# A rotary embedding on one core: two loads in halves, and VectorE's code on a block boundary

## The chip, the core and the metric

The kernel runs on one of the eight cores of a Trainium2 chip. A core has five engines that run their own instruction streams beside each other: TensorE (PE, matrix products), VectorE (DVE), ScalarE (ACT), GpSimd (POOL) and SyncE (SP, which here only issues transfers). Data moves between the chip's main memory (HBM) and the core's working memory (SBUF, 128 partitions) through 16 DMA engines that all queues share. The metric is the time of one execution on the device, in microseconds (us).

## What is computed

Each vector of 64 numbers is split into two halves, and the halves are rotated by a table of cosines and sines that depends on the position in the sequence:

```python
x: (8, 2048, 8, 64) float32;  cos, sin: (2048, 32) float32
x1, x2 = x[..., :32], x[..., 32:]
out1 = x1 * cos - x2 * sin
out2 = x1 * sin + x2 * cos
out = concatenate([out1, out2], axis=-1)
```

Input and output are 33.55 MB each, and each number is used once.

## The kernel before

The eight batches are numbered b0 to b7. One batch is a tile `xt` of 128 partitions with 8,192 numbers (32 KB) each: partition q holds 16 consecutive positions (`ROW`). A `UNIT` is a quarter of that, 2,048 numbers or 8 KB. Five such tiles exist (`NBUF`), the result is written over the input, and the tile is stored from there.

**Loads** are issued by SP (line 67, function `load`). Batch 0 comes in three transfers of 8, 8 and 16 KB per partition, the others in one of 32 KB. Lines 77 and 78 issue the loads of b0 to b4 at the start. The load of batch b+5 is issued after batch b has been worked on (line 195), into the tile that batch b used, and so waits until batch b's store has landed. A transfer is cut into rows, one for each partition, and each of the 16 DMA engines has 8 of them.

**Stores** (line 74, function `store`) are issued by ScalarE, for b7 by SP. Batch 0 is stored in three transfers of 4, 12 and 16 KB per partition, b7 in three of 16, 8 and 8 KB, the others in one of 32 KB (function `shares`).

**Work** is done in pieces of 8 KB per partition (two of 4 KB at either end, function `pieces`). `rotate` has three kinds of piece. Kind A, the usual one: GpSimd multiplies the swapped halves by the sines (line 124, two instructions), VectorE multiplies by the cosines (line 131) and adds both (line 138). Kind B, one piece in b2, b4 and b5: the addition is done by TensorE with an identity matrix (lines 145 and 146), and ScalarE copies the result back (line 147). Kind C, one piece in b1 and b3: VectorE also does the multiplication by the sines (line 150), without GpSimd. A piece waits for the transfer that holds it, so with a batch loaded in one transfer the first piece waits for all of it.

**Order.** `keep` holds each engine's instructions in the order of the program. The framework puts the semaphores: transfers take turns on eight of them, and a transfer that reuses one waits until the one before it on that semaphore has landed.

**Code alignment.** Lines 80 and 81 pad the instruction streams of VectorE and GpSimd ahead of their first own instruction, so that it stands at slot 120 of a block of 128 instruction slots:

```python
for eng in (nc.vector, nc.gpsimd):
    keep(eng.addr_align(128, offset=120))
```

Of the kernel before, what the change touches and what calls it, by code (L numbers as in the profile page):

```python
# [10 lines left out]
def kernel(  # L11
# [7 lines left out]
    nc = tc.nc  # L19
    keep = tc.keep_in_program_order  # L20
# [8 lines left out]
    ROW = R * HD  # L29
    UNIT = 4 * HD  # L30
# [27 lines left out]
    def spans(sizes):  # L58
        lo = 0
        for n in sizes:  # L60
            yield lo, n
            lo += n

    def load(b):
        xt = xpool.tile([P, ROW], f32, tag="xt", name=f"xt{b}")
        for lo, n in spans([UNIT, UNIT, 2 * UNIT] if b == 0 else [ROW]):
            keep(nc.sync.dma_start(out=xt[:, lo : lo + n], in_=xv[b, :, lo : lo + n]))  # L67
            if b == 0 and lo == 0:
                keep(nc.sync.dma_start(out=cos_sb, in_=cos_src))
        xts[b] = xt  # L70
# [6 lines left out]
    for b in range(NBUF):  # L77
        load(b)

    for eng in (nc.vector, nc.gpsimd):  # L80
        keep(eng.addr_align(128, offset=120))
    keep(nc.gpsimd.memset(eye, 0.0))  # L82
    nc.gpsimd.affine_select(
        out=eye,
# [101 lines left out]
    for b in range(B):  # L186
        done = 0
        outs = list(spans(shares(b)))
        for lo, n in spans(pieces(b)):
            rotate(b, lo, n)  # L190
            done = lo + n
            while outs and sum(outs[0]) <= done:
                store(b, *outs.pop(0))
        if b + NBUF <= last:
            load(b + NBUF)
# [30 lines left out]
```

## Time and profile before

| | |
|---|---|
| time, median of 3 runs | 163.67 us (163.3 to 163.88) |
| the profiled execution | 163.52 us, span 161.7 us |
| busy, share of the span | VectorE 87%, GpSimd 86%, TensorE 31%, ScalarE 8% |
| moved by the DMA engines | 67.65 MB, 418 GB/s over the span |
| load of a whole batch, issue to landing | 39.3 us (median of 7) |
| store of a whole batch, issue to landing | 29.2 us (median of 6) |
| VectorE: multiplication by cosines (line 131), addition (line 138) | 2167 and 2145 ns mean |
| GpSimd: one multiplication by sines (line 124) | about 2200 ns mean |

The span reaches from the first to the last instruction of the program on the core; the execution's time has 1.8 us around it. The profile is of one execution, so its parts add up to its own 163.52 us, not to the median. "q1" and "q10" are DMA queues, "q14" is the queue over which the engines' instructions are fetched. In the busy tenths a digit is the busy share of one of 40 equal slices of the span, 9 for 90% or more. A line of the waits reads: engine and line, what it waited for, microseconds in total, number of times, the longest. A line of the timeline or of the chain reads: start in us, duration in us, engine and line; a "q" behind an engine's name is its instruction that issues a transfer.

### The profile page before, as it was taken

To read this page: it belongs to the slowest core of one execution; us is meant where nothing else is said; L and a number is where in the kernel's file an instruction comes from. 1 tells how busy PE (TensorE), PEld (TensorE's weight loads), DVE (VectorE), ACT (ScalarE), POOL (GpSimd) and SP (SyncE) were. 2 spreads that over 40 slices of the span, in tenths; PEclk is the share of its full clock that TensorE was granted. 3 is DMA by queue.
4 is the path that set the end of the run, shared out by engine and by line. 5 is a ranking of instruction groups with operands and counts; after the bars stand their busy time and mean duration, and the time that the engine had idled before them with its cause. 6 is when DMAs were issued, how large, how long until landed. Compare 5 with 4: busy or idle time off the path is not lost.

```text
span 161.7 us, 565 instructions
## 1 busy us (share of the span) xinstructions
PE 50.1 (31%) x80; PEld 18.7 (12%) x80; DVE 140.1 (87%) x66; ACT 12.8 (8%) x14; POOL 138.9 (86%) x70
## 2 busy tenths in 40 slices
PE   0000000597309760978049724973000000000000
PEld 0000000142004220322023302320000000000000
DVE  0397999999999999999999999599989998999910
ACT  3300000002200220021100220022000000000000
POOL 1499996999999999995999979997999979999400
PEclk9999999999975998579956995599655555555555
DMA  5999999999999999999999999999999999999894
GB/s 181 421 434 450 411 429 425 414 417 483 393 405 454 450 446 397 454 446 397 454 446 397 446 454 397 446 454 397 454 446 397 446 454 397 454 454 421 385 422 207
DMA packets 3458, 67.65 MB, mean 418 GB/s; under 512 B 384, under 2 KB 384, under 8 KB 768
## 3 DMA queue, kind: packets, MB, share of 16 engines
q1 hardware_dynamic: 2016, 38.01, 55.4%
q10 hardware_dynamic: 1440, 29.62, 42.7%
q14 instruction: 2, 0.02, 0.0%
HBM read 34.08 MB, written 33.55 MB: 418 GB/s over the span
## 4 chain that ended last, share of the span: by engine, by line
DMA 47%; DVE 37%; POOL 9%; issue 2%; DVEq 0%; SPq 0%; POOLq 0%; ACTq 0%
DMA xt<-in_x_dram 24%; DMA out_dram<-xt 19%; DVE t L131 18%; DVE xt L138 17%; POOL t L124 9%; DMA sin_sb<-in_sin_dram 3%; DVE t L150 1%; DVEq L138 0%; SPq L67 0%; POOLq L124 0%; ACTq L74 0%
## 5 line engine op out<-in xcount | busy, mean ns | idle before, releaser
L124 POOL TENSOR_TENSOR t<-xt,sin_sb 128x1024 f32<-128x1024 f32 (+1 forms) x32 | 70.5, 2202 | 9.7 <-DMA xt<-in_x_dram 6.6
L131 DVE TENSOR_TENSOR t<-xt,cos_ps 128x2048 f32<-128x2048 f32 (+1 forms) x34 | 73.4, 2167 | 0.8
L124 POOL TENSOR_TENSOR t<-xt,nsin 128x1024 f32<-128x1024 f32 (+1 forms) x32 | 70.4, 2201 | 0.0
L138 DVE TENSOR_TENSOR xt<-t,t 128x2048 f32<-128x2048 f32 (+1 forms) x29 | 62.2, 2145 | 6.5 <-POOL t L124 4.0
L145 PE MATMUL o<-t,eye 128*128 128x512 f32 x24 | 17.5, 818 | 22.6 <-DVE t L131 19.2
L162 PE MATMUL o<-t,eye 128*128 128x512 f32 x16 | 12.2, 853 | 37.5 <-DVE t L131 35.3
L146 PE MATMUL o<-t,eye 128*128 128x512 f32 x24 | 14.9, 709 | 0.0
L147 ACT COPY xt<-o 128x1024 f32<-128x1024 f32 x6 | 6.1, 1012 | 45.7 <-PE o L146 45.7
L145 PEld LDWEIGHTS o<-t,eye 128*128 128x128 f32 x24 | 5.6, 256 | 32.0 <-issue 26.1
L162 PEld LDWEIGHTS o<-t,eye 128*128 128x128 f32 x16 | 3.7, 256 | 43.1 <-issue 39.1
L167 ACT COPY xt<-o 128x1024 f32<-128x1024 f32 x4 | 4.0, 1012 | 47.9 <-PE o L163 47.9
L146 PEld LDWEIGHTS o<-t,eye 128*128 128x128 f32 x24 | 5.7, 239 | 8.5 <-issue 8.0
L95 DVE COPY cos_ps<-cos_sb 128x512 f32<-128x512 f32 x1 | 0.7, 694 | 6.8 <-DMA cos_sb<-in_cos_dram 6.8
L163 PE MATMUL o<-t,neye 128*128 128x512 f32 x8 | 6.4, 894 | 0.2 <-DVE t L150 0.2
L150 DVE TENSOR_TENSOR t<-xt,sin_ps 128x2048 f32<-128x2048 f32 x2 | 4.6, 2282 | 0.0
L163 PE MATMUL o<-t,eye 128*128 128x512 f32 x8 | 4.1, 592 | 0.0
L163 PEld LDWEIGHTS o<-t,neye 128*128 128x128 f32 x8 | 2.2, 305 | 5.4 <-issue 3.8
L82 POOL MEMSET eye<- 128x128 f32 x1 | 0.2, 204 | 2.4 <-issue 2.4
L163 PEld LDWEIGHTS o<-t,eye 128*128 128x128 f32 x8 | 1.5, 190 | 1.9 <-issue 1.9
L92 ACT ACT_TABLE_LOAD x1 | 1.3, 1283 | 1.2 <-PEq L210 1.2
L92 ACT ACTIVATE nsin<-sin_sb 128x512 f32<-128x512 f32 x1 | 0.6, 630 | 3.9 <-DMA sin_sb<-in_sin_dram 3.9
L93 ACT COPY sin_ps<-sin_sb 128x512 f32<-128x512 f32 x1 | 0.6, 578 | 0.0
(6 smaller groups left out, 1.0 us busy)
## 6 DMA issues: line engine op xcount, KB each, us to landing
xt<-in_x_dram SPq DMA_DIRECT2D x7, 4096.0 KB, 39.3
out_dram<-xt ACTq DMA_DIRECT2D x6, 4096.0 KB, 29.2
xt<-in_x_dram SPq DMA_DIRECT2D x2, 1024.0 KB, 6.5
xt<-in_x_dram SPq DMA_DIRECT2D x1, 2048.0 KB, 12.7
out_dram<-xt ACTq DMA_DIRECT2D x1, 2048.0 KB, 26.6
out_dram<-xt SPq DMA_DIRECT2D x1, 2048.0 KB, 11.6
out_dram<-xt SPq DMA_DIRECT2D x2, 1024.0 KB, 8.0
out_dram<-xt ACTq DMA_DIRECT2D x1, 1536.0 KB, 21.5
```

The lines of the kernel that those rows point to most:

```text
L92: keep(nc.scalar.mul(nsin, sin_sb, -1.0))
L95: keep(nc.vector.tensor_copy(cos_ps, cos_sb))
L124: nc.gpsimd.tensor_mul(out=t2u[:, :, u, :].rearrange("p (r h) d -> p r h d", h=H), in0=xu[:, :, 1 - u, :].rearrange("p (r h) d -> p r h d" ...
L131: nc.vector.tensor_mul(out=t1.rearrange("p (r k d) -> p r k d", r=nr, d=Dh), in0=xk, in1=rep(cos_ps[:, r0 : r0 + nr, :], 2 * H),)
L138: keep(nc.vector.tensor_add(out=xt, in0=t1, in1=t2))
L145: nc.tensor.matmul(oc, eye, t1[:, cs], start=True, stop=False)
L146: nc.tensor.matmul(oc, eye, t2[:, cs], start=False, stop=True)
L147: keep(nc.scalar.copy(xt[:, 2 * j * C : 2 * (j + 1) * C], o))
L150: nc.vector.tensor_mul(out=t2.rearrange("p (r k d) -> p r k d", r=nr, d=Dh), in0=xk, in1=rep(sin_ps[:, r0 : r0 + nr, :], 2 * H),)
L162: nc.tensor.matmul(oc, eye, t1u[:, gs, u, :], start=True, stop=False)
L163: nc.tensor.matmul(oc, eye if u else neye, t2u[:, gs, 1 - u, :], start=False, stop=True)
L167: nc.scalar.copy(xu[:, :, u, :], o.rearrange("p (g d) -> p g d", d=Dh))
```

## The change

The loads of the second and third batch (b1 and b2) become two transfers each, one for the first and one for the second half of each partition's 32 KB, in this order on the same queue. The pieces of these batches are the same as before. VectorE's first own instruction is put at the start of a block of 128 slots instead of slot 120; GpSimd's stays at slot 120.

```diff
+    def fills(b):
+        if b == 0:
+            return [UNIT, UNIT, 2 * UNIT]
+        if b in (1, 2):
+            return [2 * UNIT, 2 * UNIT]
+        return [ROW]
+
     def load(b):
         xt = xpool.tile([P, ROW], f32, tag="xt", name=f"xt{b}")
-        for lo, n in spans([UNIT, UNIT, 2 * UNIT] if b == 0 else [ROW]):
+        for lo, n in spans(fills(b)):
             keep(nc.sync.dma_start(out=xt[:, lo : lo + n], in_=xv[b, :, lo : lo + n]))
...
-    for eng in (nc.vector, nc.gpsimd):
-        keep(eng.addr_align(128, offset=120))
+    keep(nc.vector.addr_align(128))
+    keep(nc.gpsimd.addr_align(128, offset=120))
     keep(nc.gpsimd.memset(eye, 0.0))
```

## The prediction

> **What bounds the kernel.** I read four views in this order: busy tenths and DMA queues, the chain of waits in order of time, the waits, the timeline of the last stretch. The queues first:
>
> ```profile
> DMA  5999999999999999999999999999999999999894
> ...
> q1 hardware_dynamic: 2016, 38.01, 55.4%
> q10 hardware_dynamic: 1440, 29.62, 42.7%
> q14 instruction: 2, 0.02, 0.0%
> ```
>
> The 16 DMA engines are busy in every slice, and the two queues together fill 98.1% of 16 engines' span. q1 is SP's (all loads and the last batch's stores), q10 ScalarE's (the sin load and the other stores). In the trace's list of DMA packets, rows run from 1.75 us until 160.55 with no idle time; the last store lands at 160.87. So the bytes set the end. VectorE (87%) and GpSimd (86%) follow the loads, as the chain shows:
>
> ```profile
> 93.30 39.25 DMA xt<-in_x_dram
> ...
> 132.69 4.62 POOL t L124 x2
> ...
> 137.33 2.30 DVE xt L138
> ...
> 153.03 1.23 DVE xt L138
> ```
>
> The eighth batch (b7; batches count from 0) lands at 132.55. Two GpSimd multiplies follow, then VectorE is busy to 154.26, when the last store can be issued:
>
> ```profile
> 154.28 0.33 SPq L74 DMA_DIRECT2D out_dram<-xt  x1
> ```
>
> It lands 6.6 us later, though it is 1 MB. The three last stores land at 155.99, 158.44 and 160.87: the last queued behind the other two. Without a queue it would take: issue to first row 1.0 us (first x load: issued 0.74, first row 1.75), 8 rows per engine at 0.305 = 2.44, and 0.32 from last row to landing, so 3.8 us, landing at 158.0. **Compute thus has 160.87 - 158.0 = 2.8 us of slack at the end, and no more.**
>
> GpSimd's waits say that compute hangs on the loads in the second half:
>
> ```profile
> POOL t L124 <- DMA xt<-in_x_dram: 6.6, 5, 2.2
> DVE xt L138 <- POOL t L124: 4.0, 5, 1.7
> ```
>
> **How the queues share the engines.** The packet list has a row as one packet. Medians: 2 KB 84 ns, 4 KB 159, 8 KB 309, 12 KB 460, 16 KB 611, 32 KB 1213; neighbours overlap by about 4 ns. When both queues have work an engine alternates, one row from each, whatever the sizes. Each transfer is 8 rows per engine. Batch 0's stores have rows of 4, 12 and 16 KB; the loads beside them have 32 KB, so a load gets more of the bytes. Check: the second load's first row starts at 13.65 on average. Then 8 x (1.209 + 0.155) = 10.9, 8 x (1.209 + 0.456) = 13.3 and 8 x (1.209 + 0.607) = 14.5 put the end of the fourth load at 52.4; the mean landing is 53.6, less 0.32, 53.3. The 0.9 us between are rows that ran longer than their median, 0.51 of it between 18 and 26 us.
>
> **Part 1: rows of 16 KB.** Two 16 KB rows cost 2 x 611 - 1213 = 9 ns more than one of 32 KB. Two batches of 8 rows per engine: 16 x 9 = 0.14 us on every engine, and two more semaphore packets of 9 ns. Nothing hides it: **+0.16 us**. SP issues two more transfers, 0.35 to 0.55 us each; the loads behind them (x3, x4) are first read by the engines after 40 us, so that is covered by over 20 us. Transfers reuse eight semaphores (SP waits 3.2 us on the sin load, 7.6 on an earlier x load, for this). Two more transfers shift who waits for whom by two places; the latest thing that an upfront load could then wait for is the second batch's first half (about 20.5) or the first store (about 20). It is still over 20 us early. The two halves bring about four more semaphore waits on GpSimd and VectorE, some 0.03 us each, all before 62 us; VectorE's delay there is swallowed by queued stores.
>
> **Part 2: stores get ahead, loads fall behind.** Beside rows of 16 KB the small stores get twice the turns per loaded byte. Loads b1, b2 and batch 0's stores: 32 x 0.607 + 8 x (0.155 + 0.456 + 0.607) = 29.2, so the fourth load (x3) starts at 13.65 + 29.2 = 42.8, or 43.3 with half of the 0.9 above; batch 0's last store is done at about 41, where it landed at 54.3 before. But b1's store is not issued sooner, because VectorE works without a gap from 15.94 on:
>
> ```profile
> 46.20 0.34 ACTq L74 DMA_DIRECT2D out_dram<-xt  x1
> ```
>
> From issue to first row on busy engines it took 4.2 us (first store, 10.20 to a mean of 14.40) and 4.6 (store of 144.38, mean 148.95); 4.4 gives 50.6. By then x3 has run (50.6 - 43.3) / 1.209 = 6 of its 8 rows alone. From there both queues have 32 KB rows and alternate, so every later load ends two store rows later: 2 x 1.209 + 0.16 = **2.6 us**. An engine that lags by 0.8 us has three rows left: 3.8. The slowest engine decides a landing. So b4 lands at about 77 (74.5 before; GpSimd waits 4.7 instead of 2.2) and b7 at 135.1 to 136.3. GpSimd's 1.5 us wait for b1 at 25 us goes, and brings nothing, as VectorE is late next and was never waiting there.
>
> The end by compute: 154.28 + 2.6 + 3.8 = **160.7**; with three rows 161.9. The slack of 2.8 us is just about used up. GpSimd has no reserve to catch up: it waits for each load from b4 on.
>
> **Part 3: VectorE's code at the boundary.** The packet list has two instruction packets (the 2 of q14) of 8,192 bytes, at 9.89 and 16.28. They took 0.31 and 0.32, and the row behind each ran 0.32 and 0.66 too long: 0.6 and 1.0 us on one engine each. The last 16 semaphore packets land from 159.70 to 160.87; the second last is 160.46. The late engine is probably the one with the packet of 16.28, which I take for VectorE's, as it reaches its eighth instruction past slot 120 at 11.5, later than GpSimd. At the boundary VectorE fetches before its first instruction. If that falls before 1.75 us, when rows begin, the engine gains up to 1.0 and the end **0.41** (to the second last); if it falls among the first rows it gains nothing. GpSimd, with the same kind of padding, starts its first own instruction at 2.81, so I take half: **-0.2 us**. VectorE's padding itself is hidden: its first instruction waits for the cos load until 6.81. Not below nothing: if the fetch moved to a worse place, +0.3.
>
> The Trainium skill ("Runtime: NRT & Kernel Launch", section "Instruction fetch mechanics") says that blocks are fetched ahead while the engine runs on and that crossing a block is mostly hidden. VectorE shows indeed no gap at either packet; what the page doesn't count is the queue it shares with full engines. By the page this term is zero, and the sum 0.2 us higher.
>
> **Part 4: the long rows.** 0.51 us per engine went to 32 KB load rows between 18 and 26 us, beside 4 KB stores. 16 KB rows ran at 611 flat before that, but mostly alone. Bounds: the loss goes (-0.5) or happens again as much for the next mix of sizes (+0.5). I take 0.
>
> **Sum.** By the engines 160.87 + 0.16 - 0.2 = 160.8; by compute 160.7 to 161.9. The later counts: about 160.9 to 161.1 against 160.87, so the profiled 163.52 (span 161.7, 1.8 around it) becomes 163.5 to 163.75. The median before is 163.67, 0.15 above the profiled one. **Forecast 163.7: no change**, own range 163.2 to 164.15.
>
> **Rivals.** *Slower: compute becomes the end.* If x3 has three or four rows left on the slow engines when b1's store comes in, b7 lands 3.8 to 5.0 us later and the last store is issued at 158.1 to 159.3. It lands at 161.9 to 163.1, so 164.6 to 165.8, likeliest 164.7. It decides from 2.8 us of lateness on. For it: landings go by the slowest of 16, whose spread was 2.0 us for b7. Against: the mean engine has two rows left.
>
> *Faster: both engine losses go.* The instruction packet leaves the stream (-0.41) and the long rows with it (-0.5), with +0.16: 163.67 - 0.75 = 162.9. It needs b7 to land no more than about 2 us late. For: both losses are in the trace. Against: compute must end sooner than part 2 says.
>
> *The halves don't do what they say*: if the first multiplies of b1 waited for both halves anyway, nothing here changes, since no gain is counted for it; batch 0 is already read in parts (GpSimd starts at 6.43 and its last part lands at 14.81).
>
> **Numbers.** About 0.3% (0.5 us) is what a measurement of this kernel can tell from no change. No change 0.45 (163.7), compute as the end 0.33 (164.7), losses gone 0.22 (162.9). The range takes in both rivals' likeliest: 162.8 to 164.9, with 165.8 left out.
>
> **What will show it.** q1 has 2,304 packets instead of 2,016 (128 more rows and 16 more semaphores for each batch). Batch 0's last store lands near 41. b4 to b7 land 2.6 to 3.8 us later (part 2); if they land at the old times, part 2 is wrong. The last store's issue stands near 157 and its time to landing near 3.8 to 4.2 (6.6 before): that is slack used up; below 3.9 with idle engines before it, compute is the end. One instruction packet between 2 us and 160 instead of two, and the last two semaphore packets of the last store close together (part 3). No GpSimd wait near 25 us. The forecast falls if the engines show idle time before 155 us, or if VectorE waits for code.

## The result, and the profile after

The changed kernel takes 165.03 us (median of 6, 164.8 to 165.19) against 163.69 us before (median of 6); the ratio is 1.0088, with a 95% interval of 1.0078 to 1.0098. One of the six runs before took 170.75 us in a slower state and is left out of the ratio. The loss is 1.3 us, close to the rival called "compute becomes the end" (164.7) and just above the range given. The profiled execution took 165.09 us, 1.57 more than that of before.

The page of the changed kernel, the DMA row of the 40 slices and the queues:

```profile
DMA  5999999999999999999999999999999999999966
...
q1 hardware_dynamic: 2304, 38.01, 55.5%
q10 hardware_dynamic: 1440, 29.62, 42.2%
q14 instruction: 2, 0.02, 0.0%
```

The bytes are the same and q1 has 288 packets more, as worked out. New is the end: the last two slices hold 6 tenths each, where before they held 9 and 4. The DMA engines now pause ahead of the last store. The chain that ended last, in order of time (start, duration, what):

```profile
62.42 26.48 DMA out_dram<-xt
...
89.02 47.77 DMA xt<-in_x_dram
...
136.93 4.62 POOL t L131 x2
...
141.57 2.30 DVE xt L145
...
157.27 1.23 DVE xt L145
```

(Line 131 is the line 124 of before, 138 is 131, 145 is 138, 74 is 67 and 81 is 74.) The load of b7 is issued 4.3 us earlier than before (89.02 instead of 93.30), because its tile's store, that of b2, has landed earlier. But it takes 47.8 us instead of 39.3 and lands at 136.79 instead of 132.55. Everything behind it has the same length as before and is 4.24 us later. The last store, in the timeline:

```profile
158.53 0.33 SPq L81 DMA_DIRECT2D out_dram<-xt  x1
```

It lands at 162.38, 3.85 us after its issue; before it took 6.6. So it no longer queues behind other stores: the engines wait for it. The groups of DMA issues by size (count, KB each, median us to landing) show who gained and who lost:

```profile
out_dram<-xt ACTq DMA_DIRECT2D x6, 4096.0 KB, 24.9
xt<-in_x_dram SPq DMA_DIRECT2D x5, 4096.0 KB, 47.8
```

The whole-batch stores got faster (29.2 before) and the whole-batch loads slower (39.3, over seven loads). The waits of GpSimd and VectorE, and the longest of them in the timeline, that for b4:

```profile
POOL t L131 <- DMA xt<-in_x_dram: 10.4, 5, 5.5
...
DVE xt L145 <- POOL t L131: 8.4, 6, 3.3
```

```profile
78.84 2.33 POOL L131 TENSOR_TENSOR t<-xt,sin_sb 128x1024 f32<-128x1024 f32 x1 [5.53 <-DMA xt<-in_x_dram]
```

Both waits grew by about 4 us. GpSimd's wait for b1 near 25 us is gone, and nothing became earlier by it: b1's store is issued when it was before (46.20):

```profile
46.17 0.34 ACTq L81 DMA_DIRECT2D out_dram<-xt  x1
```

### The profile page after: what moved, and what is told of

Its sections match the earlier page's. It is cut to its first block, busy times and chain, and to the rows that moved or that the text cites. A ratio compares the mean times of both kernels' runs of the same rounds, so it can differ in the third digit from the quotient of the medians.

```text
span 163.3 us, 579 instructions
## 1 busy us (share of the span) xinstructions
PE 47.2 (29%) x80; PEld 17.8 (11%) x80; DVE 140.1 (86%) x66; ACT 12.8 (8%) x14; POOL 138.9 (85%) x70
## 4 chain that ended last, share of the span: by engine, by line
DMA 49%; DVE 37%; POOL 9%; issue 2%; DVEq 0%; SPq 0%; ACTq 0%; POOLq 0%
DMA xt<-in_x_dram 29%; DVE t L138 18%; DVE xt L145 17%; DMA out_dram<-xt 16%; POOL t L131 9%; DMA sin_sb<-in_sin_dram 3%; DVE t L157 1%; DVEq L145 0%; SPq L74 0%; ACTq L81 0%; POOLq L131 0%
## 5 line engine op out<-in xcount | busy, mean ns | idle before, releaser
L152 PE MATMUL o<-t,eye 128*128 128x512 f32 x24 | 16.7, 782 | 26.6 <-DVE t L138 23.2
L169 PE MATMUL o<-t,eye 128*128 128x512 f32 x16 | 10.5, 746 | 38.5 <-DVE t L138 36.3
L153 PE MATMUL o<-t,eye 128*128 128x512 f32 x24 | 14.8, 703 | 0.0
L152 PEld LDWEIGHTS o<-t,eye 128*128 128x128 f32 x24 | 5.3, 247 | 35.9 <-issue 29.8
L169 PEld LDWEIGHTS o<-t,eye 128*128 128x128 f32 x16 | 3.5, 245 | 43.8 <-POOL t L131 30.0
L153 PEld LDWEIGHTS o<-t,eye 128*128 128x128 f32 x24 | 5.7, 238 | 8.0 <-issue 7.5
L170 PE MATMUL o<-t,eye 128*128 128x512 f32 x8 | 4.1, 592 | 0.0
L170 PEld LDWEIGHTS o<-t,eye 128*128 128x128 f32 x8 | 1.5, 190 | 1.9 <-issue 1.9
## 6 DMA issues: line engine op xcount, KB each, us to landing
xt<-in_x_dram SPq DMA_DIRECT2D x5, 4096.0 KB, 47.8
```

The source lines that it names most:

```text
L152: nc.tensor.matmul(oc, eye, t1[:, cs], start=True, stop=False)
L153: nc.tensor.matmul(oc, eye, t2[:, cs], start=False, stop=True)
L169: nc.tensor.matmul(oc, eye, t1u[:, gs, u, :], start=True, stop=False)
L170: nc.tensor.matmul(oc, eye if u else neye, t2u[:, gs, 1 - u, :], start=False, stop=True)
```

## The experiments

**The theory** (late load): the halves let batch 0's stores get ahead; b1's store then comes in while the fourth load still has rows left; all later loads end that many store rows later; the slack of compute at the end, 2.8 us, is used up. **The rivals**: each added row or transfer has a price (price per row), or VectorE's code placement costs the time (alignment).

### Each part alone

The loads in halves with the old alignment (run e1):

```diff
-    keep(nc.vector.addr_align(128))
-    keep(nc.gpsimd.addr_align(128, offset=120))
+    for eng in (nc.vector, nc.gpsimd):
+        keep(eng.addr_align(128, offset=120))
```

> Halves without the move of VectorE's code (slot 120 kept). Late-load theory: b1's store comes in with two or three rows of the fourth load left, the last batch lands 3.8 to 4.3 us later than before (136.3 to 136.8), the last store is issued at 158 to 158.6 and lands 3.85 later: 164.6 to 165.1, as the whole change. Alignment theory: the cost belongs to the code's place, so 163.7 to 163.9. One instruction packet at 7.4 in the changed kernel should be back near 16.3.

Measured: 164.74 us, ratio 1.0067 (1.0048 to 1.0086). b7 lands at 136.44, the last store is issued at 158.17 and lands 3.83 later.

The new alignment with whole loads, the other part of the diff alone (run e2):

> VectorE's code at the boundary, loads whole. Late-load theory: last batch lands as before (132.5), the DMA engines set the end, 163.3 to 163.8; the instruction packet only moves from 16.3 to about 7.4 and still delays one engine. Alignment theory: 164.5 to 165.1.

Measured: 163.37 us, ratio 0.9991 (0.9978 to 1.0003). The instruction packets are at 7.59 and 10.46. The landing of b7 missed the 132.5 expected:

```profile
92.72 41.50 DMA xt<-in_x_dram
```

It lands at 134.23, 1.7 us later than before. That is one engine of the 16 (the others are done by 132.5), it stays within the 2.8 us of slack, and the time shows nothing of it. So the halves make the loss. By itself the alignment makes no difference that can be told; on top of the halves it is at most the 0.3 us between 164.74 and 165.03, and the intervals of these two ratios overlap.

### One batch in halves

In the kernel with halves and old alignment, first the second batch alone (run e3):

```diff
-        if b in (1, 2):
+        if b == 1:
```

> Only the second batch in halves, slot 120 kept. Late-load theory: batch 0's stores are still all done before b1's store comes in, and the same bytes have gone by then, so the lateness is the same as with both: last batch at 136 to 137, 164.6 to 165.1. Price-per-row theory (each halved batch costs the same): half of the loss, 164.3 to 164.4.

Measured: 164.58 us, ratio 1.0036 (1.0011 to 1.0061); eight of ten runs took 164.4 to 165.2, two 163.2 to 163.3. By its time alone this run fits half the loss as well. Its trace doesn't: b7 lands at 136.92, as late as with both halved:

```profile
90.04 46.88 DMA xt<-in_x_dram
```

The third batch alone (run e4):

```diff
-        if b in (1, 2):
+        if b == 2:
```

> Only the third batch in halves, slot 120 kept. Late-load theory: as with the second batch alone, last batch at 136 to 137, 164.6 to 165.1; the two single edits each cost the whole loss. Price-per-row theory: 164.3 to 164.4.

Measured: 165.03 us, ratio 1.0073 (1.0043 to 1.0104); two of ten runs took 163.3 and 163.6. b7 lands at 136.74. One halved batch costs what two cost, so there is no price per row or per transfer of this size.

In both traces a single engine makes this landing. The other 15 are done with b7 by 135.04 (e3) and 135.06 (e4), 2.5 us after the 132.55 of before, which is within the slack. A run in which no engine falls a row behind would thus keep the old time, as two runs in ten did. This fits, but it isn't shown: no trace of such a run was taken.

### The same lateness without a half load

The kernel before, with fewer and larger stores of batch 0 (run e6):

```diff
         if b == 0:
-            return [2 * HD, UNIT + 2 * HD, 2 * UNIT]
+            return [2 * HD, 3 * UNIT + 2 * HD]
```

> The kernel before with all loads whole and VectorE at slot 120, but batch 0 stored in two transfers (4 and 28 KB per partition) instead of three. Late-load theory: batch 0's stores take 16 turns instead of 24, b1's store comes in with about two rows of the fourth load left, the last batch lands 3.6 to 4.3 us late, 164.6 to 165.1, with fewer rows than before and no half loads. Price-per-row theory: 163.6 or less.

Measured: 164.61 us, ratio 1.0062 (1.0042 to 1.0082). The chain of waits of this run, its last load:

```profile
88.94 47.42 DMA xt<-in_x_dram
```

The same 47 us as in the changed kernel, with fewer rows than before and every load whole. b7 lands at 136.36. This rules the price per row out: what counts is how many turns batch 0's stores take before b1's store comes in.

### The balance restored

The changed kernel, with batch 0 stored in five transfers (run e5):

```diff
         if b == 0:
-            return [2 * HD, UNIT + 2 * HD, 2 * UNIT]
+            return [2 * HD, 2 * HD, UNIT, UNIT, UNIT]
```

> The changed kernel, and batch 0 stored in five transfers (4, 4, 8, 8, 8 KB per partition) instead of three (4, 12, 16), so that as many store rows stand beside the five transfers of b1 to b3 as there are load rows. Late-load theory: stores no longer get ahead, b1's store comes in when the fifth load begins, the last batch lands at 132.5 to 133.3 and the last store waits in the queue again: 163.6 to 164.0, though there are still more rows and transfers. Price-per-row theory: 165.0 or more.

A miss: 166.64 us, ratio 1.019 (1.0172 to 1.0208); four of six runs took 166.4 to 166.8, two 168.5 and 168.9, and the trace is of the longest. Twelve of the 16 engines land b7 about when expected: their packets come from 129.7 to 132.9. The other four come at 136.7 to 136.9. In the trace's packet list, store rows, mostly four at a time, took up to 1.9 us instead of 1.21 again and again from 64 to 93 us, so that four engines fell about 5 us behind and were still the last at the end (165.8 to 166.0, against 162.3 to 162.5 for the other twelve). So this run says nothing for or against the theory at the end of the kernel; what slowed these rows stays open. The same count of turns with other row sizes (run e10):

```diff
-            return [2 * HD, UNIT + 2 * HD, 2 * UNIT]
+            return [2 * HD, UNIT + 2 * HD, UNIT, 2 * HD, 2 * HD]
```

> The changed kernel with batch 0 stored in five transfers of 4, 12, 8, 4, 4 KB per partition (4, 4, 8, 8, 8 had four engines whose store rows ran 0.6 us too long between 64 and 93 us, on a landing that was otherwise in time). Late-load theory: as many store turns as load turns up to b1's store, the mean landing of the last batch goes back to 131 to 132.5 us; if the long rows stay away, 163.6 to 164.1; if they come again on four engines, 166 or more, with the mean landing still early. Price-per-row theory: 165 or more with a mean landing at 135.

Measured: 164.23 us, ratio 1.0041 (1.0025 to 1.0057), just above the range expected. No store row of 32 KB took over 1.3 us. b7 lands at 129.98, its 16 packets at 127.3 on average, earlier than in the kernel before and than expected: the last 4 KB store lands only at 58.8 and b1's store begins at 58.5, behind it. GpSimd's waits for loads are nearly gone, and the last store's issue is early again:

```profile
POOL t L131 <- DMA xt<-in_x_dram: 0.5, 1, 0.5
```

```profile
152.39 0.33 SPq L81 DMA_DIRECT2D out_dram<-xt  x1
```

It lands at 161.52, 9.1 us later, so the DMA engines set the end again. Its 16 packets come at 160.33 on average, 0.20 later than before (160.13), which is about the price that the prediction put on the added rows. The last packet is 0.48 behind the second last, and why that engine is late is not shown. So with the loads in halves and no late load, the kernel is still not faster than before.

### Is compute the end?

The changed kernel (run e7) and the kernel before (run e8), each without the rotation of the last piece, so that these two leave out a part of the result:

```diff
-            rotate(b, lo, n)
+            if not (b == last and lo + n == ROW):
+                rotate(b, lo, n)
```

> The changed kernel without the rotation of the very last piece (the last 4 KB per partition of b7 are stored as loaded), so that the last store can be issued 2.5 us earlier; all transfers stay. Late-load theory: compute was the end, so the last store is issued at about 156, and the end falls back to the DMA engines': 163.5 to 164.0. If the DMA engines had set the end of the changed kernel: 165.0.

Measured: 163.84 us, ratio to the kernel before 1.0015 (1.0002 to 1.0029). b7 lands as late as in the changed kernel (136.63), but VectorE's last instruction ends at 155.74:

```profile
154.51 1.23 DVE xt L145
```

The last store is issued at 155.76 and lands at 161.20, after 5.4 us.

> The kernel before without the rotation of the very last piece (the last 4 KB per partition of b7 are stored as loaded). Late-load theory: the DMA engines set the end, so 163.4 to 163.8, no change, although VectorE ends 2.5 us earlier. If compute had been the end before too: about 161.2.

Measured: 163.70 us, ratio 1.0004 (0.9993 to 1.0015). The same 2.5 us of VectorE's work is worth nothing before the change and 1.2 us after it. So of the 1.34 us of loss some 1.2 is compute past the DMA engines' end; the engines' own part is 0.25 us by e7's ratio (0.03 to 0.47).

### How much slack there was

The kernel before, with VectorE's multiplication of the last piece done three times (run e11, shown) and five times (run e12):

```diff
-        keep(
-            nc.vector.tensor_mul(
...
+        for _ in range(3 if b == last and lo + n == ROW else 1):
+            keep(
+                nc.vector.tensor_mul(
```

> The kernel before, and VectorE does the last piece's multiplication by the cosines three times instead of once (two more of about 1.24 us), so that the last store is issued some 2.5 to 2.7 us later; no transfer changes. If compute has 2.8 us of slack at the end of the kernel before: 163.5 to 163.9, no change, the last store 3.9 to 4.2 us from issue to landing. If it has none: 166.2.

Measured: 163.50 us, ratio 0.9993 (0.9981 to 1.0005). The last store in the timeline:

```profile
156.83 0.33 SPq L74 DMA_DIRECT2D out_dram<-xt  x1
```

2.55 us later than before, and it lands at 160.71, 3.88 after its issue: the slack is just used, at no price.

> The kernel before, and VectorE does the last piece's multiplication by the cosines five times instead of once, so that the last store is issued some 5.0 to 5.4 us later. With 2.8 us of slack: only what is over it shows, 2.2 to 2.6 us, 165.9 to 166.3, the last store 3.85 us from issue to landing. With no slack 168.8; with the DMA engines as the only bound 163.7.

Measured: 165.84 us, ratio 1.0141 (1.0118 to 1.0165).

```profile
159.41 0.33 SPq L74 DMA_DIRECT2D out_dram<-xt  x1
```

5.13 us later, landing 3.84 after; the time rose by 2.25. So 5.13 - 2.25 = 2.9 us were free (2.4 to 3.2 by the interval), where the prediction said 2.8.

### Can the instruction packets be moved out of the way?

The kernel before, with both paddings at another slot (run e9):

```diff
-        keep(eng.addr_align(128, offset=120))
+        keep(eng.addr_align(128, offset=16))
```

> The kernel before with both code paddings at slot 16 instead of 120, so that both bodies fit the rest of a block of 128 slots. If the packets of 9.9 and 16.3 are asked for as the code crosses the boundary, they now come while the padding runs, before 3 us, and the end, set by the latest engine, comes up to 0.4 us earlier: 163.2 to 163.6. If they are asked for only by the first instructions that wait for data, as in the changed kernel (7.4), nothing is gained: 163.5 to 163.8.

Measured: 163.51 us, ratio 1.0002 (0.9991 to 1.0013). The packets come at 6.82 and 7.78, about when the two engines begin their first data instructions, and still beside the loads.

## Why the prediction was wrong, point by point

**What bounds the kernel, and the slack: right.** The DMA engines set the end before (e8), and compute had 2.8 us (2.9 measured, e11 and e12). From issue to landing without a queue 3.8 us were reckoned and 3.83 to 3.88 measured.

**Part 1, rows of 16 KB, +0.16 us: right in size.** The engines' end moved by 0.25 us (0.03 to 0.47) in e7 and by 0.20 in e10's mean landing.

**Part 2, "every later load ends two store rows later: 2 x 1.209 + 0.16 = 2.6 us": this step failed.** Up to it the numbers held: the fourth load's first row starts at 43.6 (43.3 reckoned), batch 0's last store lands at 41.4 (41), b1's store has its first row at 50.57 on average (50.6), and 5.75 rows of the fourth load have started by then (6). But the landings of b7 are 3.83 us later on average (135.06 against 131.23), the last one 4.24. The packet list shows the missing row. In order of time most engines run, from the fourth load (x) and b1's store (s):

```
x x x x x x s x s x s s x ...
```

The fourth load's eighth row is the tenth in this order, two store rows late as worked out. But what tells the waiting engine is the load's semaphore packet, and it takes a turn of its own: a store row runs ahead of it, hence two s in a row. So on these engines a load is reported three store rows late, 3 x 1.209 + 0.16 = 3.79, against 3.83 measured on average. In the kernel before, load and batch 0's store ended together on most engines, and the turn ahead of the packet went to batch 0's last row, whose bytes are in the old landing times already. The prediction counted rows and left the packet behind the last one out.

The landing itself goes by the slowest engine. In the changed kernel four of the 16 engines had run five rows of the fourth load, not six, when b1's store came in, and are one row later than the others: their packets for this load come at 58.5 to 59.4, those of the twelve at 57.0 to 57.5. In the kernel before, three engines already had a row of b1's store ahead of the packet (54.7 to 55.1, the others 53.1 to 54.1). From slowest to slowest it is thus again three rows, 3.79; the other 0.45 of the 4.24 measured has no shown cause. These four engines set the time: for b7 the twelve are done by 134.97, 2.4 us after the 132.55 of before and within the slack, the four at 135.9 to 136.8. The prediction had this case, "an engine that lags by 0.8 us has three rows left: 3.8", and the rule that the slowest engine decides, but its sum went on with 2.6.

**Part 3, alignment, -0.2 us: the step was wrong, the size can't be told from nothing.** The packet that the prediction expected to vanish from the stream only moved from 16.28 to 7.40, among the rows of batch 0. With whole loads the alignment is worth between 0.36 us faster and 0.05 slower (e2), which holds both -0.2 and zero. The last packet of the last store is still 0.50 behind the second last there (0.41 before), so the engine's gain did not come. The Trainium skill ("Runtime: NRT & Kernel Launch", section "Instruction fetch mechanics"), which calls the crossing of a block mostly hidden, agrees with this as far as e2 can tell, though each packet occupies a DMA engine for 0.31 us.

**Part 4, long rows, 0: right.** 0.51 us per engine between 18 and 26 us before, 0.55 after, though the rows there are now 16 KB.

**The sum.** "By compute 160.7 to 161.9" and "the later counts" were the right form, but the forecast was taken from the low end, 160.9 to 161.1. That end adds two store rows to the landing; the slowest engine was 4.24 us late, which gives 154.28 + 4.24 + 3.85 = 162.37 against 162.38 measured. With its own 161.9, for an engine with three rows left, the sum would have come to 164.7. That is the rival "compute becomes the end", which had 0.33 and named three or four rows left on the slow engines as its condition: four engines had three left.

## What to carry to other kernels

When loads and stores share DMA engines that are always full, ask which queue gets the turns, not only how many bytes there are: in this kernel a transfer's row size and count decided its share, and loads in 16 KB rows let batch 0's last store land at 41.4 instead of 54.3. Compute the landing of the last load for the slowest engine, count the semaphore packet as a turn, and compare the lateness with the slack between the last store's issue and the queue ahead of it: 2.55 us within the slack cost nothing (e11), and of 5.13 all beyond it showed (e12). Of the versions tried none beats the kernel before: its balance, batch 0's stores ending with the fourth load, already kept the DMA engines busy up to the last store.

## What the runs showed of the hardware that was not expected

- In the changed kernel a semaphore packet of 4 bytes takes 9 ns by itself, but waits for its turn behind a whole row of the other queue: 1.21 us with rows of 32 KB.
- Four of the 16 engines can fall behind the others for good: in e5 their store rows took up to 1.9 us instead of 1.21 between 64 and 93 us, and they ended at 165.8 to 166.0 against 162.3 to 162.5. Other sizes of the same stores (e10) had none of it. The cause is open.
- The engines' instruction packets, 8,192 bytes each, come among the data rows at each of the three alignments tried: 6.8 and 7.8 us in e9, 7.6 and 10.5 in e2, 9.9 and 16.3 in the kernel before.
